# Low parts of four weight quarters in branch B computed on GpSimd instead of VectorE

## Chip, core and metric

One core of one Trainium2 chip runs the whole kernel. Times are device microseconds (us) of one execution; the number compared is the median over runs. TensorE is called PE, VectorE DVE, ScalarE ACT, GpSimd POOL; SP is the engine that only issues transfers here.

## The reference, cut to what matters

A mixer layer over 512 tokens of width 1024: one wide projection of the normalized input gives twelve blocks of 1024 columns, three branches (A: gated chunk mixing, B: window pooling, C: short convolution) use them, each branch is projected, gated and summed, and a last projection and norm follow.

```python
h = rmsnorm(x, norm_g[l])
proj = jnp.einsum('bsd,dn->bsn', h, w_in[l])
a_u, a_v, a_z, b_p, b_z, c_h, c_b, c_c, c_z, gate_logits = jnp.split(proj, SPLIT_OFFSETS, axis=-1)
...
yb = multiscale_pool(b_p, pool_w[l], pool_b[l], pool_scale[l]) * jax.nn.silu(b_z)
...
gates = jax.nn.sigmoid(gate_logits.reshape(bsz, s, N_BRANCH, D_MODEL))
merged = (gates[:, :, 0] * jnp.einsum('bsc,cd->bsd', ya, w_branch_a[l])
          + gates[:, :, 1] * jnp.einsum('bsc,cd->bsd', yb, w_branch_b[l])
          + gates[:, :, 2] * jnp.einsum('bsc,cd->bsd', yc, w_branch_c[l]))
```

## The kernel before

Everything is kept transposed, channels in partitions and tokens along the free dimension. Float32 accuracy comes from splitting each operand in a high part, which ACT makes by a rounding copy, and a low part, the difference between operand and high part, which DVE makes (`split`, lines 57 to 60). A product then takes three matmuls: high by high, high weights by low activations, low weights by high activations.

Most blocks of w_in are multiplied in `group` (lines 426 to 495), 512 output columns at a time, by a scheme of the Strassen kind with seven instead of eight quarter products. A group loads four weight quarters of 512 rows by 256 columns (tiles of 128x1024: a11, a12, a21, a22) and, in s1, the sum of two quarters, which an accumulating transfer from the POOL queue makes (line 469). DVE forms differences of quarters in place (line 457). The seven products, named by the activation form that they use, come in this order: b11, b21, t2, t1, t3, then b22 (from a12) and t4 (from a22, the quarter as loaded). Each is 24 matmuls at line 444 (2 column halves x 4 row blocks x 3 parts); within one row block the low weight part comes last in the code. `halved` (line 434) takes a high tile and a low tile, each from a pool of four, and calls `split`.

`run` (line 497) lets groups overlap: the first product of a group is issued before b22 and t4 of the group ahead of it. Branch B's list (lines 731 to 736) is: pool_in(1) with the window sums pools(1) behind it, pool_z(0), pool_mms(0), pool_z(1), gates(0), pool_mms(1), mixes(0), gates(1), mixes(1). pools (line 665) is DVE work: repeated shifted adds (line 677), a scaled difference (line 680), a short correction (lines 683 and 684), and a split. pool_mms multiplies by pool_w (lines 105 to 107) and ends in an epilogue on DVE and ACT (lines 706 to 709) whose results are needed in mixes. The results of a group are collected by DVE from PSUM (line 454) and by ACT (lines 450 and 524).

Only instructions wrapped in `pin` keep the order of the code. All others are ordered on each engine by a planner before the run, by the order of the code and by when it reckons each to be ready. Transfers of weights are issued by SP in its own order (line 64), seven raw weight tiles being in turn.

Of the kernel before, what the change touches and what calls it, by code (L numbers as in the profile page):

```python
# [8 lines left out]
F32 = mybir.dt.float32  # L9
F32R = mybir.dt.float32r  # L10
AF = mybir.ActivationFunctionType
ALU = mybir.AluOpType
# [14 lines left out]
OFF = {n: i * D for i, n in enumerate(["au", "av", "az", "bp", "bz", "ch", "cb", "cc", "cz", "g0", "g1", "g2"])}  # L27
# [3 lines left out]
def mixers_kernel(ctx, tc, x, norm_g, w_in, sgu_ln_g, sgu_ln_b, sgu_w, sgu_b, pool_w, pool_b, pool_scale,  # L31
                  conv_w, conv_b, w_branch_a, w_branch_b, w_branch_c, w_out, final_g, out):
    nc = tc.nc
# [20 lines left out]
    def bank():  # L54
        return psum.tile([P, 512], F32, tag="ps", name="ps")

    def split(hi, lo, src, keep=lambda ins: ins):

        keep(nc.scalar.copy(out=hi, in_=src))  # L59
        keep(nc.vector.tensor_tensor(out=lo, in0=src, in1=hi.bitcast(F32), op=ALU.subtract))  # L60

    def load_raw(src, shape):
        raw = wraw.tile([P, *shape], F32, tag="wraw", name="wraw")
        nc.sync.dma_start(out=raw, in_=src)
        return raw
# [8 lines left out]
    def cols(w2d, c0):  # L74

        v = w2d[:, c0 : c0 + GC].rearrange("(k p) c -> p k c", p=P)
        units = [load_w(v[:, 4 * h : 4 * h + 4, :], [4, GC]) for h in range(2)]

        def at(k, j):
            hi, lo = units[k // 4]  # L80
            return hi[:, k % 4, j * P : (j + 1) * P], lo[:, k % 4, j * P : (j + 1) * P]

        return at
# [319 lines left out]
    def proj(w, j, rhs_hi, rhs_lo, nk=KT):  # L403
        ps = bank()
        for k in range(nk):
            mm3(ps, w(k, j), (rhs_hi[:, k, :], rhs_lo[:, k, :]), k == 0, k == nk - 1)
        return ps

    def tile512(name):
        return tmp.tile([P, PAD + S], F32, tag="tmp", name=name)[:, 0:S]  # L410

    def out_tile(name):

        return outs.tile([P, 2, 2, S], F32, tag="outs", name=name)
# [8 lines left out]
    def pair_of(ap):  # L423
        return ap.rearrange("p (j t) -> p j t", j=2)

    def group(c0, g, ct, use=None):
        def source(kh, nh):
            c = c0 + nh * HALF + g * GC
            return w_in[kh * HALF : (kh + 1) * HALF, c : c + GC].rearrange("(k p) c -> p k c", p=P)

        def quarter(kh, nh):
            return load_raw(source(kh, nh), [4, GC])

        def halved(raw):
            hi = whi.tile([P, 4, GC], F32R, tag="whi", name="whi")
            lo = wlo.tile([P, 4, GC], F32R, tag="wlo", name="wlo")
            split(hi, lo, raw)
            return hi, lo

        def product(a, b, ps, first):  # L440
            for j in range(2):
                for k in range(4):
                    for n, (x, y) in enumerate([(0, 0), (0, 1), (1, 0)]):
                        nc.tensor.matmul(ps[:, j * GC : (j + 1) * GC], lhsT=a[x][:, k, j * P : (j + 1) * P],  # L444
                                         rhs=moving[b][y][:, k, :], start=first and j == 0 and k == 0 and n == 0,
                                         stop=k == 3 and n == 2, skip_group_check=True)

        def copied(ps):
            s = part.tile([P, S], F32, tag="part", name="part")
            nc.scalar.copy(out=s, in_=ps)  # L450
            return pair_of(s)

        def plus(half, ts, s, ps):
            nc.vector.tensor_tensor(out=ct[:, half, :, ts], in0=pair_of(ps), in1=s, op=ALU.add)  # L454

        def sub(out, in0, in1, op=ALU.subtract):
            nc.vector.tensor_tensor(out=out, in0=in0, in1=in1, op=op)  # L457

        a11 = quarter(0, 0)
        f = halved(a11)  # L460
        px, py, pz = bank(), None, None
        product(f, "b11", px, True)
        yield
        c1 = copied(px)
        a12 = quarter(1, 0)
        f = halved(a12)
        s1 = wsum.tile([P, 4, GC], F32, tag="wsum", name="s1")
        nc.sync.dma_start(out=s1, in_=source(0, 1))
        nc.gpsimd.dma_start(out=s1, in_=source(1, 1), accum_op=ALU.add)  # L469
        a21, a22 = quarter(0, 1), quarter(1, 1)  # L470
        py = bank()
        product(f, "b21", py, True)
        plus(0, T1, c1, py)
        sub(a21, a11, a21)
        sub(a11, s1, a11)
        product(halved(a11), "t2", px, False)
        c2 = copied(px)
        pz = bank()
        product(halved(s1), "t1", pz, True)
        product(halved(a21), "t3", px, False)  # L480
        c3 = copied(px)
        sub(a12, a12, a11)
        plus(1, T2, c3, pz)
        yield
        product(halved(a12), "b22", pz, False)
        plus(0, T2, c2, pz)
        if use:
            use(ct[:, 0], 0, slice(0, S))
            use(ct[:, 1, :, T2], 1, T2)
        product(halved(a22), "t4", px, False)  # L490
        if use:
            use(pair_of(px), 1, T1)
        else:
            nc.scalar.copy(out=ct[:, 1, :, T1], in_=pair_of(px))
        yield
# [26 lines left out]
    def act_into(ct, func):  # L522
        def use(src, half, ts):
            nc.scalar.activation(out=ct[:, half, :, ts], in_=src, func=func)
        return use
# [52 lines left out]
    def m_quarter(k, th):  # L578
        return merged[:, 4 * k : 4 * k + 4, th * GC : (th + 1) * GC]

    def form(name, src):

        m_form[name] = form_tile("m", f"f{len(m_form)}")
        split(*m_form[name], src)
# [8 lines left out]
    def merge(br, w_branch):  # L593

        state = {}

        def gates(g):
            state[g] = out_tile("gate")
            yield from group(OFF[f"g{br}"], g, state[g], act_into(state[g], AF.Sigmoid))

        def mixes(g):
            wb = {}

            def mix(t):
                if t % 2 == 0:
                    wb[t // 2] = cols(w_branch, t * P)
                return proj(wb[t // 2], t % 2, y_hi, y_lo)

            def under(t, ps):
                nonlocal merged  # L610
                if merged is None:
                    merged = acts.tile([P, KT, S], F32, tag="big", name="merged")
                gate = state[g][:, t // 4, t % 2]
                if br == 0:
                    nc.vector.tensor_mul(out=merged[:, t, :], in0=ps, in1=gate)
                    return
                pr = tile512("pr")
                nc.vector.tensor_mul(out=pr, in0=ps, in1=gate)
                nc.vector.tensor_add(out=merged[:, t, :], in0=merged[:, t, :], in1=pr)
                if br == 2 and g == 1 and t == 3:  # L620
                    form("b11", m_quarter(0, 0))
                    minus(m_quarter(0, 0), m_quarter(0, 0), m_quarter(0, 1))
                    form("-t1", m_quarter(0, 0))

            first = mix(TILES[g][0])

            def after():
                under(TILES[g][0], first)
                for t in TILES[g][1:]:
                    under(t, mix(t))  # L630

            return after

        for g in range(2):
            items.append(("group", gates(g), None))
            items.append(("other", lambda g=g: mixes(g)))
# [4 lines left out]
    def make_pads():  # L641
        for i in range(2):
            pads.append(const.tile([P, 2, PAD + S], F32, tag=f"pad{i}", name=f"ppad{i}"))
            nc.gpsimd.memset(pads[i][:, :, 0:PAD], 0.0)
# [11 lines left out]
    silu_z = {}  # L656

    def pool_in(g):
        if not pads:
            make_pads()  # L660
        yield from group(OFF["bp"], g, Padded())

    early = {}

# [26 lines left out]

    def pool_z(g):
        silu_z[g] = out_tile("sz")
        yield from group(OFF["bz"], g, silu_z[g], act_into(silu_z[g], AF.Silu))

    def pool_mm(p):
        hi, lo = load_w(pool_w[0, p].rearrange("(k p) c -> p k c", p=P), [2, GC])
# [130 lines left out]
    def product(units, name, pss, first):  # L828
        for b in range(2):
            for k in range(4):  # L830
                hi, lo = units[k // 2]
                for n, (x_, y_) in enumerate([(0, 0), (0, 1), (1, 0)]):
                    nc.tensor.matmul(pss[b], lhsT=m_form[name][x_][:, k, b * P : (b + 1) * P],  # L833
                                     rhs=(hi, lo)[y_][:, k % 2, :], start=first and k == 0 and n == 0,
                                     stop=k == 3 and n == 2, skip_group_check=True)
# [34 lines left out]
    px, pz = banks(), banks()  # L870
# [54 lines left out]
```

## Time and profile before

| | us |
|---|---|
| median of 3 runs | 702.45 |
| lowest and highest | 701.51, 703.87 |
| the profiled execution | 701.71 |
| its span | 699.9 |
| PE busy | 684.6 (98%) |
| DVE busy | 530.6 (76%) |
| ACT busy | 343.3 (49%) |
| POOL busy | 53.4 (8%) |

The span is the stretch from the first to the last instruction of the profiled execution; the rest of its time lies around it. PE's clock was granted in full (9 tenths or more in all but the last of the 40 slices). The rows of a timeline give start, duration, engine, line, operation, output and inputs, and in brackets how long the engine had been idle before and what ended that. An instruction's duration can reach a little into the next one's on the same engine.

### The profile page before, as it was taken

The numbers are of one execution on the slowest core, as the hardware profiler recorded it, in microseconds if no ns is written. First come the engines' busy times: TensorE is split into PE (matmuls) and PEld (weight loads), VectorE is DVE, ScalarE is ACT, GpSimd is POOL, SyncE is SP. The second block draws the span as 40 slices with busy tenths as digits, with TensorE's granted clock in tenths as the row PEclk, the third lists the DMA queues.
The fourth block names the chain that finished last, engine by engine and source line by source line (L and its number), as shares of the span: only waits on it lengthen the run. The fifth ranks groups of instructions, "written<-read, shape, count | busy, mean of one in ns | idle before, by whom it ended". The sixth has DMA issues, their size and how long they took to land.

```text
span 699.9 us, 11608 instructions
## 1 busy us (share of the span) xinstructions
PE 684.6 (98%) x4814; PEld 637.2 (91%) x4814; DVE 530.6 (76%) x615; ACT 343.3 (49%) x417; POOL 53.4 (8%) x68
## 2 busy tenths in 40 slices
PE   8999999999999999989999999999999999999994
PEld 6779999999899899989989899999999999898883
DVE  6997679695669667995855666798869975646995
ACT  7543546664244344655614334555645465244553
POOL 3112000000000000000000000000000000002112
PEclk9999999999999999999999999999999999999998
DMA  7974344746265434627617235556665543278733
GB/s 275 309 169 120 121 122 102 213 109 181 79 163 152 149 87 132 175 90 195 197 32 209 91 104 167 149 144 167 176 168 163 163 140 124 81 270 189 149 60 121
DMA packets 94457, 105.12 MB, mean 150 GB/s; under 512 B 3324, under 2 KB 85316, under 8 KB 94404
## 3 DMA queue, kind: packets, MB, share of 16 engines
q1 hardware_dynamic: 80020, 87.60, 38.9%
q0 software_dynamic: 13792, 15.73, 14.4%
q10 hardware_dynamic: 592, 1.05, 0.4%
q8 instruction: 37, 0.61, 0.4%
q14 instruction: 16, 0.13, 0.1%
HBM read 102.27 MB, written 2.10 MB: 149 GB/s over the span
## 4 chain that ended last, share of the span: by engine, by line
PE 89%; DVE 5%; DMA 2%; ACT 1%; issue 1%; POOL 0%; SPq 0%; POOLq 0%; ACTq 0%; DVEq 0%
PE ps L444 58%; PE ps L106 8%; PE ps L107 8%; PE ps L105 8%; PE ps L833 5%; PE ps L265 2%; DVE wlo L60 1%; DMA x_in<-in_x 1%; DVE win L677 1%; DMA wraw<-in_w_in 1%; DVE wraw L457 1%; PE ps L563 1%; PE ps L215 0%; DVE sz L454 0%; DVE ylo L709 0%
## 5 line engine op out<-in xcount | busy, mean ns | idle before, releaser
L59 ACT CAST whi<-wraw 128x1024 fp32r<-128x1024 f32 (+1 forms) x174 | 180.6, 1040 | 262.0 <-PE ps L444 160.2
L60 DVE TENSOR_TENSOR wlo<-wraw,whi 128x1024 fp32r<-128x1024 f32 (+1 forms) x174 | 209.6, 1210 | 95.6 <-ACT whi L59 95.3
L105 PE MATMUL ps<-yhi,whi 128*128 128x512 f32 x208 | 81.0, 389 | 0.0
L107 PE MATMUL ps<-yhi,wlo 128*128 128x512 f32 x208 | 80.9, 389 | 0.0
L106 PE MATMUL ps<-ylo,whi 128*128 128x512 f32 x208 | 80.9, 389 | 0.0
L457 DVE TENSOR_TENSOR wraw<-wraw 128x1024 f32<-128x1024 f32 x44 | 53.4, 1220 | 16.3 <-DMA wraw<-in_w_in 16.3
L469 POOL DMA_DIRECT2D s<-in_w_in x22 | 28.8, 1308 | 482.1 <-DMA s<-in_w_in 81.9
L444 PE MATMUL ps<-b22h,whi 128*128 128x256 f32 x176 | 50.6, 288 | 0.5 <-DVE sz L454 0.5
L444 PE MATMUL ps<-b21h,wlo 128*128 128x256 f32 x176 | 49.4, 280 | 1.2 <-DVE wlo L60 1.2
L444 PE MATMUL ps<-t2h,wlo 128*128 128x256 f32 x176 | 49.4, 281 | 0.5 <-DVE wlo L60 0.5
L444 PE MATMUL ps<-t1h,whi 128*128 128x256 f32 x176 | 49.4, 281 | 0.4 <-ACT whi L59 0.4
L444 PE MATMUL ps<-t2h,whi 128*128 128x256 f32 x176 | 49.5, 281 | 0.1
L444 PE MATMUL ps<-t2l,whi 128*128 128x256 f32 x176 | 49.6, 282 | 0.0
L444 PE MATMUL ps<-b11l,whi 128*128 128x256 f32 x176 | 49.6, 282 | 0.0
L444 PE MATMUL ps<-t3l,whi 128*128 128x256 f32 x176 | 49.6, 282 | 0.0
L444 PE MATMUL ps<-t1l,whi 128*128 128x256 f32 x176 | 49.6, 282 | 0.0
L444 PE MATMUL ps<-b22l,whi 128*128 128x256 f32 x176 | 49.6, 282 | 0.0
L444 PE MATMUL ps<-t4l,whi 128*128 128x256 f32 x176 | 49.6, 282 | 0.0
L444 PE MATMUL ps<-b21l,whi 128*128 128x256 f32 x176 | 49.6, 282 | 0.0
L444 PE MATMUL ps<-t3h,whi 128*128 128x256 f32 x176 | 49.3, 280 | 0.0
L444 PE MATMUL ps<-b22h,wlo 128*128 128x256 f32 x176 | 49.3, 280 | 0.0
L444 PE MATMUL ps<-b21h,whi 128*128 128x256 f32 x176 | 49.3, 280 | 0.0
(224 smaller groups left out, 1849.6 us busy)
## 6 DMA issues: line engine op xcount, KB each, us to landing
wraw<-in_w_in SPq DMA_DIRECT2D x96, 512.0 KB, 4.0
s<-in_w_in SPq DMA_DIRECT2D x22, 512.0 KB, 3.6
s<-in_w_in POOLq DMA_DIRECT2D x22, 512.0 KB, 6.3
wraw<-in_w_out SPq DMA_DIRECT2D x10, 512.0 KB, 3.8
wraw<-in_w_branch_a SPq DMA_DIRECT2D x8, 512.0 KB, 3.7
wraw<-in_w_branch_b SPq DMA_DIRECT2D x8, 512.0 KB
wraw<-in_w_branch_c SPq DMA_DIRECT2D x8, 512.0 KB
wraw<-in_w_out POOLq DMA_DIRECT2D x8, 512.0 KB, 6.0
```

Source lines behind the costliest of these rows:

```text
L59: keep(nc.scalar.copy(out=hi, in_=src))
L60: keep(nc.vector.tensor_tensor(out=lo, in0=src, in1=hi.bitcast(F32), op=ALU.subtract))
L105: nc.tensor.matmul(ps, lhsT=a[0], rhs=b[0], start=first, stop=False)
L106: nc.tensor.matmul(ps, lhsT=a[0], rhs=b[1], start=False, stop=False)
L107: nc.tensor.matmul(ps, lhsT=a[1], rhs=b[0], start=False, stop=last)
L265: pin(nc.tensor.matmul(vps[b], lhsT=a, rhs=r, start=done[b] == 1, stop=done[b] == 3 * KT))
L444: nc.tensor.matmul(ps[:, j * GC : (j + 1) * GC], lhsT=a[x][:, k, j * P : (j + 1) * P], rhs=moving[b][y][:, k, :], start=first and j == 0 a ...
L457: nc.vector.tensor_tensor(out=out, in0=in0, in1=in1, op=op)
L469: nc.gpsimd.dma_start(out=s1, in_=source(1, 1), accum_op=ALU.add)
L563: nc.tensor.matmul(mx[:, n * P : (n + 1) * P], lhsT=v_t[:, n, t * P : (t + 1) * P], rhs=wsT[:, t, :], start=True, stop=True)
L677: nc.vector.tensor_add(out=nxt[:, lo:], in0=cur[:, lo:], in1=cur[:, lo - step : PAD + S - step])
L833: nc.tensor.matmul(pss[b], lhsT=m_form[name][x_][:, k, b * P : (b + 1) * P], rhs=(hi, lo)[y_][:, k % 2, :], start=first and k == 0 and n == 0,
```

## The change

`split` takes an engine for the subtraction, DVE where none is named. `group` takes a `helper`, which goes to the split of a22 alone, the quarter of product t4. Four groups name GpSimd: gates(0) of branch B, pool_in(1), pool_z(0) and pool_z(1). All other splits, all shapes, buffers and values stay as they are.

```diff
-    def split(hi, lo, src, keep=lambda ins: ins):
+    def split(hi, lo, src, keep=lambda ins: ins, eng=None):
 
         keep(nc.scalar.copy(out=hi, in_=src))
-        keep(nc.vector.tensor_tensor(out=lo, in0=src, in1=hi.bitcast(F32), op=ALU.subtract))
+        keep((eng or nc.vector).tensor_tensor(out=lo, in0=src, in1=hi.bitcast(F32), op=ALU.subtract))
...
-    def group(c0, g, ct, use=None):
+    def group(c0, g, ct, use=None, helper=None):
...
-        def halved(raw):
+        def halved(raw, eng=None):
             hi = whi.tile([P, 4, GC], F32R, tag="whi", name="whi")
             lo = wlo.tile([P, 4, GC], F32R, tag="wlo", name="wlo")
-            split(hi, lo, raw)
+            split(hi, lo, raw, eng=eng)
             return hi, lo
...
-        product(halved(a22), "t4", px, False)
+        product(halved(a22, helper), "t4", px, False)
...
-            yield from group(OFF[f"g{br}"], g, state[g], act_into(state[g], AF.Sigmoid))
+            yield from group(OFF[f"g{br}"], g, state[g], act_into(state[g], AF.Sigmoid),
+                             helper=nc.gpsimd if br == 1 and g == 0 else None)
...
-        yield from group(OFF["bp"], g, Padded())
+        yield from group(OFF["bp"], g, Padded(), helper=nc.gpsimd if g else None)
...
-        yield from group(OFF["bz"], g, silu_z[g], act_into(silu_z[g], AF.Silu))
+        yield from group(OFF["bz"], g, silu_z[g], act_into(silu_z[g], AF.Silu), helper=nc.gpsimd)
```

## Rows read from the trace of the kernel before

**Rows 1.** The page: busy time by engine; the chain that ended last, by engine.

```profile
PE 684.6 (98%) x4814; PEld 637.2 (91%) x4814; DVE 530.6 (76%) x615; ACT 343.3 (49%) x417; POOL 53.4 (8%) x68
...
PE 89%; DVE 5%; DMA 2%; ACT 1%; issue 1%; POOL 0%; SPq 0%; POOLq 0%; ACTq 0%; DVEq 0%
```

**Rows 2.** Table by stage: stretch, length, busy us (instructions) of each engine, clock, transfers.

```profile
273.00:300.00 27.00, 27.00 (x210) 26.05 (x209) 26.93 (x47) 16.06 (x22) 1.29 (x1) 1.00 0.55 154
300.00:307.00 7.00, 4.79 (x34) 3.96 (x33) 6.93 (x9) 4.56 (x6) 0.00 (x0) 1.00 0.00 0
...
316.00:340.00 24.00, 24.00 (x193) 23.34 (x192) 15.06 (x17) 14.34 (x19) 1.29 (x1) 1.00 0.84 218
...
sum 632.00, PE 629.11 PEld 593.06 DVE 477.76 ACT 305.39 POOL 39.23; mean PE 78.64 PEld 74.13 DVE 59.72 ACT 38.17 POOL 4.90
```

**Rows 3.** Timeline of PE, 291 to 312 us: start, duration, engine, line, operation.

```profile
291.85 0.28 PE L444 MATMUL ps<-t4h,whi 128*128 128x256 f32 x1
...
297.40 0.28 PE L444 MATMUL ps<-b11h,whi 128*128 128x256 f32 x1
...
300.22 0.28 PE L444 MATMUL ps<-b21h,whi 128*128 128x256 f32 x1
...
301.86 0.39 PE L444 MATMUL ps<-b21h,wlo 128*128 128x256 f32 x1 [1.24 <-DVE wlo L60]
...
305.69 0.39 PE L444 MATMUL ps<-t1h,whi 128*128 128x256 f32 x1 [0.43 <-ACT whi L59]
...
306.69 0.38 PE L444 MATMUL ps<-t2h,wlo 128*128 128x256 f32 x1 [0.49 <-DVE wlo L60]
...
311.98 0.28 PE L444 MATMUL ps<-t3h,whi 128*128 128x256 f32 x1
```

**Rows 4.** Timeline of DVE, 261 to 306 us.

```profile
261.81 1.23 DVE L60 TENSOR_TENSOR wlo<-wraw,whi 128x1024 fp32r<-128x1024 f32 x1 [0.35 <-ACT whi L59]
264.63 1.23 DVE L60 TENSOR_TENSOR wlo<-wraw,whi 128x1024 fp32r<-128x1024 f32 x1 [1.59 <-ACT whi L59]
...
283.81 1.23 DVE L60 TENSOR_TENSOR wlo<-wraw,whi 128x1024 fp32r<-128x1024 f32 x1
...
285.55 1.23 DVE L60 TENSOR_TENSOR wlo<-wraw,whi 128x1024 fp32r<-128x1024 f32 x1
286.69 0.70 DVE L680 SCALAR_TENSOR_TENSOR d<-win,ppad 128x512 f32<-128x512 f32 x1
...
288.08 0.69 DVE L454 TENSOR_TENSOR sz<-ps,part 128x512 f32<-128x512 f32 x1
...
295.36 0.75 DVE L706 SCALAR_TENSOR_TENSOR y<-ps,pvec,sz 128x512 f32<-128x512 f32 x1
...
300.59 1.22 DVE L60 TENSOR_TENSOR wlo<-wraw,whi 128x1024 fp32r<-128x1024 f32 x1
...
305.42 1.22 DVE L60 TENSOR_TENSOR wlo<-wraw,whi 128x1024 fp32r<-128x1024 f32 x1
```

**Rows 5.** Timeline of ACT, two casts of pool_z(0).

```profile
280.78 1.05 ACT L59 CAST whi<-wraw 128x1024 fp32r<-128x1024 f32 x1 [2.26 <-PE ps L444]
...
283.59 1.05 ACT L59 CAST whi<-wraw 128x1024 fp32r<-128x1024 f32 x1 [0.76 <-ACT part L450]
```

**Rows 6.** Timeline of POOL: its subtraction, two pow operations, two accumulating loads.

```profile
12.79 2.40 POOL L236 TENSOR_TENSOR wlo<-wraw,whi 128x1024 fp32r<-128x1024 f32 x1 [0.54 <-ACT whi L232]
15.15 0.55 POOL L152 TENSOR_TENSOR rstd<-ms,mhalf 128x1 f32<-128x1 f32 x1
19.74 1.46 POOL L152 TENSOR_TENSOR rstd<-ms,mhalf 128x1 f32<-128x1 f32 x1 [4.04 <-DVE ms L199]
...
279.27 1.29 POOL L469 DMA_DIRECT2D s<-in_w_in  x1 [18.80 <-DMA s<-in_w_in]
313.66 1.30 POOL L469 DMA_DIRECT2D s<-in_w_in  x1 [33.09 <-DVE wraw L457]
```

**Rows 7.** Timeline of DVE at the second of these pow operations.

```profile
19.58 1.22 DVE L337 TENSOR_TENSOR hsum<-b21h,b21l 128x1024 f32<-128x1024 f32 x1
```

## The prediction

> **What bounds the kernel now.** I read the page's busy shares and its chain first, then PE by stage, then the one stage in which PE stands still. PE is busy 98% of the span and carries 89% of the chain that ended last; DVE carries 5% of it [rows 1]. The table by stage makes this sharp: from 20 to 652 us PE is busy 629.11 of 632 us, so 2.9 us of idle time is all there is, and 2.21 of it (7.00 less 4.79) lies between 300 and 307 us [rows 2]. There DVE is the engine that is late: it is busy 26.93 of the 27 us before and 6.93 of the 7 us of the hole [rows 2]. In the code this is branch B: the window sums of pools(1) and the epilogue of pool_mms(0) run on DVE while PE goes through pool_z(0), pool_mms(0) and the start of pool_z(1).
>
> The records of PE show what the hole costs in full. In pool_z(1) product b11 starts at 297.40 and b21 at 300.22, so one product of 24 matmuls takes 2.82 us. Undisturbed, t3, four products behind b11, would start at 297.40 + 4 x 2.82 = 308.68; it starts at 311.98. The loss is 3.30 us: PE stops for the low part of b21 (301.86), for a cast (305.69) and for the low part of t2 (306.69) [rows 3]. Those low parts are DVE's operations at 300.59 and 305.42, and PE goes on within 0.05 us of their ends (300.59 + 1.22 = 301.81; 305.42 + 1.22 = 306.64) [rows 3, 4]. So DVE time spent between 273 and 305 us is worth its length in kernel time, up to 3.30 us; DVE time spent elsewhere in branch B is worth nothing, because PE is full there.
>
> **What the change takes from DVE.** Four subtractions of 128x1024, one in each of pool_in(1), pool_z(0), pool_z(1) and gates(0) of branch B. Back to back, such an operation moves DVE on by 286.69 - 285.55 = 1.14 us [rows 4]. Each has to be placed:
> - pool_in(1): weight tiles come free four products back, and counting casts against products puts its low part at 261.81 or 264.63. DVE idles 1.59 us before the second of these [rows 4], so nothing late there is made earlier: 0.
> - pool_z(0): the casts of its b22 and t4 quarters are those at 280.78 and 283.59 [rows 5]; a12 comes first in the code, so t4's low part is the DVE operation at 285.55 [rows 4]. It lies in the unbroken DVE stretch ahead of both waits: -1.14 us. This is the only one of the four that can pay.
> - pool_z(1): its t4 cast needs the weight tile of t2, which PE takes up in earnest only at 306.69 [rows 3], after the last stop: 0.
> - gates(0): in 316 to 340 us DVE is busy 15.06 of 24 us and PE all 24 [rows 2]: 0.
>
> If nothing else happened, PE would stop 3.30 - 1.14 = 2.16 us instead of 3.30.
>
> **What it adds on GpSimd.** The trace has one such subtraction on GpSimd: 2.40 us at 12.79 [rows 6], 1.18 us longer than DVE's 1.22. Does t4 of pool_z(0) wait for it? The cast at 283.59 ends at 284.64; started then, the low part is there at about 287.1. PE reads it first in t4's third matmul, 291.85 + 0.24 = 292.09 [rows 3]. Cover: 5.0 us. The other three are covered more amply, since PE reads t4 a product or more behind their casts.
>
> GpSimd's own queue carries the accumulating loads of line 469. In the stretch they stand at 279.27 and 313.66 [rows 6]; between them the queue is empty for 33 us, so the subtraction of pool_z(0) waits for none of them and none for it. The one at 313.66 may come 2.4 us later behind the subtraction of pool_z(1); what it loads is the s1 of a group two ahead, so that costs 0. The raw quarter's buffer is given back about 1.2 us later, and SP loads the next weights into it; no PE wait in the stretch comes from a load: 0.
>
> **What GpSimd does to DVE** is the open price, and it decides the sign. Rows of before: GpSimd's one-element pow at 15.15 takes 0.55 us, the one at 19.74 takes 1.46 us [rows 6]; under the second, DVE runs a subtraction with both inputs in SBUF from 19.58 to 20.80 [rows 7], and GpSimd ends 0.40 us behind it. So GpSimd's reads wait for such a DVE operation. Whether DVE waits as well when GpSimd came first no row shows: under the 2.40 us at 12.79 DVE ran only operations with one input in PSUM. Bounds: at the low end DVE never waits, and the subtraction of pool_z(0) is worth -1.14. At the high end DVE waits for the whole 2.40 us, -1.14 + 2.40 = +1.26. I take a wait, because the one pair of rows that touches the question shows the two engines taking turns and not sharing. Its length: GpSimd goes on for 0.40 us after it had its data (the tail behind 20.80), so it holds DVE for 2.40 - 0.40 = 2.0 us. Behind the held instruction all of DVE's queue waits: the window sums, then the low parts of b11, b21 and t2 of pool_z(1), for which PE waits. Net on the path: -1.14 + 2.0 = +0.86 us.
>
> The Trainium skill ("SBUF — State Buffer", section "Who interferes with whom") says that a VectorE instruction with two SBUF inputs and a GpSimd instruction that reads SBUF exclude each other, and that the one that starts first keeps the other out for its whole length. The trace agrees for GpSimd kept out (1.46 against 0.55 us); for VectorE kept out no run here shows it. By that rule the sum would be +1.26 us, the high end above.
>
> The same hold can happen in the other three groups. There DVE has its own idle time, 9 of 24 us in gates(0)'s stretch [rows 2], and PE has no wait, so I put them at 0; without that cover each would cost what pool_z(0)'s does.
>
> **The sum.** The profiled execution took 701.71 us, 699.9 of span and 1.8 around it; the median of the three runs is 702.45, 0.74 above. Added to the profiled time, +0.86 gives 702.57; I add it to the median, which is what is compared: 703.3 us.
>
> **Rivals.**
> 1. DVE isn't held: -1.14, 701.3 us. For it: GpSimd may only get its reads in where DVE reads PSUM (the operation at 288.08 [rows 4] does, and 288.08 + 2.4 = 290.5 is still ahead of 292.09). Against it: the operations that follow there again have two SBUF inputs.
> 2. The planned order closes the hole: the order of DVE's work comes out of a planner, and with an operation less it may put the low part of b21 ahead of the pool epilogue (from 295.36 on [rows 4]), which PE doesn't need soon. At best all 3.30 go: 699.2 us. For it: more than 1.14 us of such movable work stands ahead of 300.59. Against it: code order put it there before, and nothing in the change alters the code order.
> 3. Slower: GpSimd is starved. DVE is back to back from 273 to 307, and nearly all of it reads two SBUF inputs. If GpSimd is kept out through 288.08 and gets in only at the pool epilogue, 295.36 [rows 4], its result is there at 295.36 + 2.40 = 297.76 and PE, which wants it at 292.09, stops for 5.67 us. DVE catches up meanwhile, so the old 3.30 us go: net +2.4, 704.8 us. It decides from the point where the low part lands later than 292.09 + 3.30 = 295.4; up to there the stop only changes its place. Against it: DVE reads PSUM at 288.08.
> 4. The change does not act on the path: pool_z(0)'s low part isn't the one at 285.55 but one outside the full DVE stretch. Then nothing moves: 702.45 us.
>
> **How the numbers follow.** Held (my forecast) 0.42; not held 0.26; hole closed 0.12; starved 0.14; no effect 0.06. A measurement of this kernel tells about 0.3% (2.1 us) from no change: the three runs span 701.51 to 703.87. Forecast, not held and no effect (0.74 together) lie within 2.1 us of 702.45, less some 0.06 that the scatter of runs carries over either bound. Faster by over 0.3% is the closed hole with a little of not held: 0.14. Slower is starvation and the upper tail of my forecast: 0.18. Same: 0.68. The range goes from 700.3 (not held, 701.3, less 1 us of run scatter; it leaves the closed hole out) to 705.8 (starved, 704.8, plus 1 us). Both signs hold much of the chance; the forecast's own range is 702.3 (hold of 1.0 us) to 704.7 (1.26 plus 1 us of scatter).
>
> **What would show it.** Right: in the table by stage PE's idle time stays in one hole of 2 to 5 us at about 300 to 308 us; GpSimd shows four 128x1024 subtractions, the second starting at about 285 and lasting 2.4 to 3.6 us; a DVE operation with two SBUF inputs beside it lasts about 2 us longer than its kind. If DVE's operations keep their lengths, rival 1 is right. If PE's longest wait is for GpSimd at t4 near 292, rival 3. If no PE wait for DVE is left and the pool epilogue stands behind the low part of b21, rival 2. The prediction is wrong in its ground if time moves in a stage before 273 or after 316 us, where I see none to gain or lose.

## The result, and the profile after

The changed kernel takes 707.97 us (median of 7 runs, 704.85 to 710.32) against 702.46 before: the ratio is 1.0066, with a 95% interval of 1.0048 to 1.0083. It is slower, by 3.4 to 5.8 us. A second measurement gave 1.0069 (1.0045 to 1.0093). The forecast was 703.3 us with a range up to 705.8. The ratios here and below leave out one execution, 749.92 us of the kernel with all but pool_z(0), whose granted clock was 0.85 on the mean.

The profiled execution took 707.97 us with a span of 706.2. First the table by stage of the changed kernel, same columns and stretches as [rows 2]:

```profile
273.00:300.00 27.00, 25.14 (x190) 24.33 (x189) 26.01 (x41) 14.14 (x18) 6.22 (x2) 0.94 0.56 157
300.00:307.00 7.00, 7.00 (x50) 6.49 (x50) 6.83 (x11) 4.26 (x7) 0.00 (x0) 1.00 0.00 0
307.00:316.00 9.00, 7.49 (x63) 7.29 (x63) 8.10 (x8) 4.93 (x6) 0.00 (x0) 1.00 0.41 133
316.00:340.00 24.00, 22.71 (x194) 22.51 (x194) 12.59 (x12) 11.51 (x14) 6.48 (x4) 1.00 0.71 172
```

Where one hole stood at 300 to 307 us, there are three: 1.86 us in the first row, 1.51 in the third, 1.29 in the fourth. In the first row PE's clock, ahead of the DMA columns, is 0.94 where it was 1.00. The timeline of PE names what ended each:

```profile
292.90 0.39 PE L444 MATMUL ps<-b22h,whi 128*128 128x256 f32 x1 [1.86 <-DVE sz L454]
...
310.74 0.39 PE L444 MATMUL ps<-t2h,wlo 128*128 128x256 f32 x1 [1.51 <-DVE wlo L60]
...
323.28 0.38 PE L444 MATMUL ps<-b22h,whi 128*128 128x256 f32 x1 [1.29 <-DVE sz L454]
```

Two of the three are for sz: the sum of line 454 (`plus(1, T2, c3, pz)`), which reads the PSUM bank that b22 then adds to. GpSimd's four subtractions, on its timeline:

```profile
266.55 2.40 POOL L60 TENSOR_TENSOR wlo<-wraw,whi 128x1024 fp32r<-128x1024 f32 x1 [4.58 <-ACT whi L59]
...
286.60 4.91 POOL L60 TENSOR_TENSOR wlo<-wraw,whi 128x1024 fp32r<-128x1024 f32 x1 [4.05 <-ACT whi L59]
...
318.62 2.91 POOL L60 TENSOR_TENSOR wlo<-wraw,whi 128x1024 fp32r<-128x1024 f32 x1
...
338.57 2.40 POOL L60 TENSOR_TENSOR wlo<-wraw,whi 128x1024 fp32r<-128x1024 f32 x1 [3.87 <-ACT whi L59]
```

And DVE at the second and the third of them:

```profile
286.82 0.68 DVE L678 TENSOR_TENSOR win<-win 128x513 f32<-128x513 f32 x1
287.42 1.22 DVE L457 TENSOR_TENSOR wraw<-wraw 128x1024 f32<-128x1024 f32 x1
288.56 0.68 DVE L681 SCALAR_TENSOR_TENSOR d<-win,ppad 128x512 f32<-128x512 f32 x1
289.16 2.38 DVE L684 TENSOR_TENSOR dh<-win,rcount 128x16 f32<-128x16 f32 x1
...
292.16 0.68 DVE L454 TENSOR_TENSOR sz<-ps,part 128x512 f32<-128x512 f32 x1
...
320.05 2.57 DVE L60 TENSOR_TENSOR wlo<-wraw,whi 128x1024 fp32r<-128x1024 f32 x1 [2.56 <-ACT whi L59]
322.54 0.68 DVE L454 TENSOR_TENSOR sz<-ps,part 128x512 f32<-128x512 f32 x1
```

In pool_z(0) GpSimd is ready at 286.60 and is kept out while three DVE operations pass; then it gets in, and the next DVE operation, 16 elements wide, lasts 2.38 us. It ends at 291.54, GpSimd at 291.51. It is the same DVE operation in all six traces in which GpSimd has pool_z(0)'s low part; why GpSimd gets in there and not earlier stays open. In pool_z(1) GpSimd starts while DVE is idle, and the DVE subtraction at 320.05 lasts 2.57 instead of 1.22 us [rows 4]. Behind each held operation stands sz, and for sz PE waits. In the other two groups GpSimd takes its 2.40 us, as in [rows 6], while DVE stands idle.

Start times of the same products in both traces give the account. The stretch from b11 of pool_in(1) to b11 of the second gates group of branch B took 367.70 - 252.17 = 115.53 us before and 372.99 - 254.03 = 118.96 after, 3.43 more:

| piece of the stretch | before | after | difference |
|---|---|---|---|
| b11 of pool_in(1) to b22 of pool_z(0) | 36.85 | 38.87 | +2.02 |
| to b11 of pool_z(1) | 8.38 | 10.05 | +1.67 |
| to t3 of pool_z(1) (the old hole) | 14.58 | 13.11 | -1.47 |
| to b22 of pool_z(1) | 5.91 | 7.22 | +1.31 |
| to b11 of the second gates group | 49.81 | 49.71 | -0.10 |

The second piece holds no wait but the fall of the clock. The table of the changed kernel in steps of 2 us shows it (the granted clock is the third number from the right; 0.50 of full speed is 1.2 GHz):

```profile
290.00:292.00 2.00, 1.04 (x5) 0.54 (x3) 2.00 (x2) 0.00 (x0) 1.51 (x1) 1.00 0.02 8
292.00:294.00 2.00, 1.10 (x9) 1.10 (x10) 2.00 (x6) 1.71 (x2) 0.00 (x0) 1.00 0.65 205
294.00:296.00 2.00, 2.00 (x13) 2.00 (x13) 2.00 (x5) 1.76 (x3) 0.00 (x0) 0.59 0.20 66
296.00:298.00 2.00, 2.00 (x12) 2.00 (x12) 2.00 (x4) 0.92 (x1) 0.00 (x0) 0.55 0.75 226
298.00:300.00 2.00, 2.00 (x19) 2.00 (x19) 2.00 (x4) 1.71 (x3) 0.00 (x0) 1.00 0.10 36
```

PE works again from 292.90 at the upper level, falls to the lower near 294.4 and is back by 298: 12 and 13 matmuls per 2 us instead of 19.

Of the 6.3 us between the two spans, 3.43 lie in this stretch, 1.86 ahead of it, 0.95 behind the last matmul (10.39 us from its start to the end, 9.44 before). The piece ahead is scatter: in the twelve traces of this study b11 of pool_in(1) started anywhere from 251.64 to 256.79 us, and at 252.26 in a second trace of the changed kernel itself. Most of it is PE's idle time between 20 and 44 us, long before the change: 1.50 us in this trace, 0.31 in the second, 0.11 in the trace of before. The piece at the end comes back below.

### The profile page after: what moved, and what is told of

Its sections match the earlier page's. It is cut to its first block, busy times and chain, and to the rows that moved or that the text cites. A ratio compares the mean times of both kernels' runs of the same rounds, so it can differ in the third digit from the quotient of the medians.

```text
span 706.2 us, 11614 instructions
## 1 busy us (share of the span) xinstructions
PE 685.6 (97%) x4814; PEld 638.1 (90%) x4814; DVE 529.5 (75%) x611; ACT 343.4 (49%) x417; POOL 65.8 (9%) x72
## 4 chain that ended last, share of the span: by engine, by line
PE 89%; DVE 4%; DMA 3%; ACT 2%; issue 1%; SPq 0%; POOL 0%; POOLq 0%; ACTq 0%; DVEq 0%
PE ps L444 59%; PE ps L106 8%; PE ps L107 8%; PE ps L105 8%; PE ps L834 5%; DMA ws_bs<-in_sgu_w 1%; DMA x_in<-in_x 1%; DVE wlo L60 1%; DMA wraw<-in_w_in 1%; PE ps L265 1%; DVE win L678 1%; PE ps L563 1%; PE ps L215 0%; DVE sz L454 0%; DMA out_y<-o 0%
## 5 line engine op out<-in xcount | busy, mean ns | idle before, releaser
L60 DVE TENSOR_TENSOR wlo<-wraw,whi 128x1024 fp32r<-128x1024 f32 x170 | 205.9, 1217 | 100.2 <-ACT whi L59 100.0
L444 PE MATMUL ps<-t4h,whi 128*128 128x256 f32 x176 | 49.5, 281 | 0.0
L444 PE MATMUL ps<-t4h,wlo 128*128 128x256 f32 x176 | 49.4, 281 | 0.0
```

The source lines that it names most:

```text
L60: keep((eng or nc.vector).tensor_tensor(out=lo, in0=src, in1=hi.bitcast(F32), op=ALU.subtract))
```

## The experiments

All read the stretch of branch B as above, in one trace each; ratios are from repeated runs.

| kernel | stretch, us | last matmul to end, us | ratio (95%) |
|---|---|---|---|
| before | 115.53 | 9.44 | 1 |
| changed | 118.96 | 10.39 | 1.0066 (1.0048 to 1.0083) |
| changed, second time | 119.34 | 10.40 | 1.0069 (1.0045 to 1.0093) |
| pool_z(0) alone | 117.68 | 9.50 | 1.0024 (1.0005 to 1.0043) |
| all but pool_z(0) | 116.27 | 9.70 | 1.0024 (1.0006 to 1.0041) |
| pool_in(1) and gates(0) | 115.54 | 9.47 | 1.0007 (0.9990 to 1.0024) |
| GpSimd only writes | 114.21 | 10.35 | 1.0000 (0.9981 to 1.0020) |
| epilogue later, no GpSimd | 112.37 | 9.47 | 0.9953 (0.9935 to 0.9971) |

**Which group costs: pool_z(0) alone.**

```diff
-             helper=nc.gpsimd if br == 1 and g == 0 else None)
+             helper=None)
-    yield from group(OFF["bp"], g, Padded(), helper=nc.gpsimd if g else None)
+    yield from group(OFF["bp"], g, Padded(), helper=None)
-    ... act_into(silu_z[g], AF.Silu), helper=nc.gpsimd)
+    ... act_into(silu_z[g], AF.Silu), helper=None if g else nc.gpsimd)
```

> Only pool_z(0) keeps its low part on GpSimd. Theory (GpSimd holds DVE): in the changed kernel DVE's tiny operation at 289.16 lasted 2.38 instead of about 0.18 us while GpSimd read, DVE's sum sz behind it came late, PE stood 1.86 us before b22, and PE's clock fell behind that. All of this is pool_z(0)'s, so most of the loss returns here: ratio 1.003 to 1.005 (2 to 3.5 us), with the long DVE operation and the PE wait for sz. Rival (the loss is spread over the groups, or comes from elsewhere in the run): about a quarter of it, ratio 1.000 to 1.002.

The stretch grew by 2.15 us, 63% of the changed kernel's 3.43; the ratio, 1.0024, lies below the 1.003 expected, and its interval is wide. The trace repeats the picture: a held operation of 2.37 us, GpSimd's subtraction 5.01 us long, PE waiting 1.95 us for sz, its clock at 0.50 between 292 and 294. So do the pieces of the table above: +2.01, +1.65, -1.49, -0.04 and +0.02 us. By the stretch the largest part is pool_z(0)'s.

**The other three.** The edit is the reverse: `helper=nc.gpsimd if g else None` for pool_z, the other two as in the change.

> The three other groups use GpSimd, pool_z(0) uses DVE. Theory: the hole of 3.3 us at 300 to 307 us is as in the kernel before, since nothing is held ahead of it; pool_z(1)'s subtraction can still hold DVE by up to 1.4 us ahead of the sum that b22 of pool_z(1) waits for: ratio 1.000 to 1.002, no fall of PE's clock. Rival (each of the four costs alike): 1.004 to 1.006.

The stretch grew by 0.74 us, all of it ahead of b22 of pool_z(1); the line of PE in that trace:

```profile
319.19 0.39 PE L444 MATMUL ps<-b22h,whi 128*128 128x256 f32 x1 [0.69 <-DVE sz L454]
```

The ratio, 1.0024, is just above the expected 1.002; what the trace shows, 0.74 us in the stretch and 0.26 at the end, would be 1.0014, inside the interval. The clock did not fall. By the ratios alone the two halves of the change cost the same, 1.0024 each; that pool_z(0) costs most rests on the stretch, in one trace of each kernel.

**The two groups in which DVE idles.** `helper=None` for pool_z, the other two as in the change.

> Only pool_in(1) and gates(0) use GpSimd, the two groups in which DVE has idle time. Theory: both are free, ratio within 0.999 to 1.001, GpSimd's two subtractions last 2.4 us each and no DVE operation beside them is longer than its kind. Rival (GpSimd at work costs wherever it stands, or later weight loads are pushed): 1.002 or more.

As expected: 115.54 us against 115.53, and no DVE operation there is longer than its kind: DVE stood idle all through GpSimd's two. GpSimd's work is free where DVE has nothing to do.

**GpSimd without its reads.** The same places and the same order; a fill stands for the subtraction.

```diff
-        keep((eng or nc.vector).tensor_tensor(out=lo, in0=src, in1=hi.bitcast(F32), op=ALU.subtract))
+        keep(eng.memset(lo.bitcast(F32), 0.0) if eng else nc.vector.tensor_tensor(out=lo, in0=src, in1=..., op=ALU.subtract))
```

> The changed kernel with GpSimd's four subtractions replaced by a fill with zeros of the same tiles: the low part of a22 is left out of the product t4 in these four groups. Waits and the order on every engine are those of the changed kernel, GpSimd only no longer reads SBUF. Theory (GpSimd's reads hold DVE): no DVE operation is lengthened, PE doesn't wait for sz, the clock stays up, and the removed DVE work shows as -1.1 us or a little more: ratio 0.997 to 1.000. Rival (the planner's new order, or the later hand-over from GpSimd to PE, makes the loss): the loss stays, 1.004 to 1.007.

The DVE order in the stretch is the changed kernel's, instruction for instruction. The waits are not quite: the fill reads no high part, so it doesn't wait for the cast, and it starts 31.41 us behind b11 of pool_in(1) where the subtraction started 32.57 behind it. The fill, the DVE subtraction beside it, the operation that was held before, and sz:

```profile
288.20 0.96 POOL L60 MEMSET wlo<- 128x1024 f32 x1 [2.64 <-PE ps L444]
...
288.43 1.22 DVE L60 TENSOR_TENSOR wlo<-wraw,whi 128x1024 fp32r<-128x1024 f32 x1
...
291.91 0.17 DVE L684 TENSOR_TENSOR dh<-win,rcount 128x16 f32<-128x16 f32 x1
...
292.69 0.69 DVE L454 TENSOR_TENSOR sz<-ps,part 128x512 f32<-128x512 f32 x1
```

0.17 instead of 2.38 us, and the DVE subtraction beside the fill takes its usual 1.22 us: the fill neither holds DVE nor is held. sz starts 35.90 us behind b11 of pool_in(1), against 35.91 before and 38.13 in the changed kernel. PE doesn't wait for sz in the stretch, the clock stays up there, and the stretch is 114.21 us, 1.32 shorter than before and 4.75 shorter than with the subtraction. So the planner's new order doesn't make the loss. Nor does the hand-over: in no trace does PE wait for GpSimd in the stretch. What is left is the subtraction. The fill is shorter (0.96 us where the subtraction takes 2.40), but it holds DVE not at all. It leaves out the arithmetic together with the reads; no run here parts these two. The ratio, 1.0000, is at the upper edge of what was expected: the end is 0.91 us longer, as in the changed kernel, and takes back most of the gain.

**Half the reads.** On the kernel with pool_z(0) alone:

```diff
+        if eng:
+            keep(eng.tensor_tensor(out=lo[:, 0:2], in0=src[:, 0:2], in1=hi[:, 0:2].bitcast(F32), op=ALU.subtract))
+            keep(eng.memset(lo[:, 2:4].bitcast(F32), 0.0))
+            return
```

> As the run with pool_z(0) alone on GpSimd, but GpSimd subtracts only half of the tile (128x512) and fills the other half with zeros: half of a22's low part is left out of t4. Order on PE, DVE and ACT as in that run. There the held DVE operation lasted 2.37 us and PE then stood 1.95 us for sz. Theory (the hold is the length of GpSimd's read, and it alone delays sz): the held operation lasts 1.2 to 1.5 us, PE's wait for sz is 0.7 to 1.1 us, and its clock falls less or not at all. Rival (a fixed price per GpSimd operation, or a wait caused by the order): 2.2 us and 1.9 us again.

Here is the held operation on DVE:

```profile
287.69 1.29 DVE L688 TENSOR_TENSOR dh<-win,rcount 128x16 f32<-128x16 f32 x1
```

and what PE waits for behind it:

```profile
290.33 0.39 PE L448 MATMUL ps<-b22h,whi 128*128 128x256 f32 x1 [0.86 <-DVE sz L458]
```

Half the subtraction gives half the hold, as expected: 1.29 against 2.37 us, and the wait falls by as much, from 1.95 to 0.86. GpSimd's subtraction still lasts 3.92 us, from 285.02 to 288.94, but for some 2.7 of them it was kept out, since the held operation starts at 287.69. DVE pays for GpSimd's work, not for its waiting, and by its length, not at a fixed price per operation. The clock stayed up, and the stretch was 115.32 us.

**The clock.** On the kernel with pool_z(0) alone, spare work for PE behind the first product of pool_mms(0):

```diff
+        if g == 0:
+            spare = bank()
+            for _ in range(9):
+                nc.tensor.matmul(spare[:, 0:P], lhsT=ones, rhs=ones, start=True, stop=True)
```

> As the run with pool_z(0) alone on GpSimd, with nine spare matmuls of 128x128 on a matrix of ones put into PE's queue between the first product of pool_mms(0) and b22, so PE works through part of its wait for sz. In that run, b22 and t4 of pool_z(0) took 5.0 plus 1.0 us more than undisturbed, because the clock fell after the wait. Theory (the fall follows PE's standing still): PE's idle time before b22 shrinks below 0.6 us, the clock stays at the upper level, and b22 runs its 24 matmuls in about 3 instead of 4.6 us. Rival (the fall has nothing to do with the wait): b22 takes 4.6 us again. Later parts aren't compared, since the planner also moves the pool epilogue here.

PE's timeline (the nine matmuls are 18 records):

```profile
289.67 2.17 PE L721 MATMUL ps<-ones 128*128 128x128 f32 x18
291.68 0.39 PE L444 MATMUL ps<-b22h,whi 128*128 128x256 f32 x1
```

and its table in steps of 2 us:

```profile
290.00:292.00 2.00, 2.00 (x19) 1.97 (x18) 2.00 (x5) 0.92 (x2) 0.29 (x1) 1.00 0.21 52
292.00:294.00 2.00, 2.00 (x19) 2.00 (x18) 2.00 (x5) 1.99 (x3) 0.00 (x0) 1.00 0.62 210
```

DVE was held for 2.38 us and b22 came just as late, 38.86 us behind b11 of pool_in(1) in both, but PE wasn't idle ahead of it, and the clock is 1.00 where it was 0.50 in the run without spare work. b22 takes 3.1 instead of 4.6 us, and from b22 to b11 of pool_z(1) pass 8.52 us instead of 10.03. So the standing still costs about 1.5 us on top of itself. (The expectation's "5.0 plus 1.0 us more" is a misreading: b22 and t4 together took 7.29 us in the run without spare work and 5.66 in the kernel before, 1.63 more.)

**The old hole.** The hole of [rows 3] was worth 3.30 us. Nothing about GpSimd is in this kernel; it is the kernel before with the epilogue of pool_mms(0) put behind t3 of pool_z(1):

```diff
         def after():
+            if g == 0:
+                waiting.extend([first, pool_mm(g + 2)])
+                return
             first()
             pool_mm(g + 2)()
...
+    def with_waiting(gen):
+        next(gen)
+        yield
+        next(gen)
+        for f in waiting:
+            f()
+        yield
+        next(gen)
+        yield
...
-              ("group", pool_z(1), None)]
+              ("group", with_waiting(pool_z(1)), None)]
```

> The kernel before, without GpSimd's help, with the epilogue of pool_mms(0) issued after t3 of pool_z(1) in the code, so that the planner puts the low parts of pool_z(1) ahead of it on DVE. Theory (the 3.3 us hole of the kernel before is DVE time spent on work that PE doesn't need yet): the hole shrinks to under 1 us, the stretch from b11 of pool_in(1) to b11 of the second gates group falls from 115.5 to 112.3 to 113.5 us, ratio 0.995 to 0.998. Rival (PSUM banks held longer by the waiting sums, or the epilogue is late for its use, makes a new wait): 0.999 to 1.003.

It is faster than both kernels: 700.01 us against 703.25 for the kernel before beside it, ratio 0.9953. PE's row for the stage of the hole, and DVE with the low part of t2 ahead of three of the four epilogue products:

```profile
300.00:307.00 7.00, 7.00 (x58) 6.84 (x58) 7.00 (x8) 4.55 (x6) 0.00 (x0) 1.00 0.15 44
```

```profile
303.44 1.21 DVE L60 TENSOR_TENSOR wlo<-wraw,whi 128x1024 fp32r<-128x1024 f32 x1
...
308.11 2.05 DVE L706 SCALAR_TENSOR_TENSOR y<-ps,pvec,sz 128x512 f32<-128x512 f32 x3
```

PE's 2.21 idle us there [rows 2] are gone, and the stretch is 3.16 us shorter. DVE does as much as before (530.3 us busy in the whole kernel, 530.6 before), only in another order.

**The changed kernel again.**

> The changed kernel once more beside the others. In its first profile the stretch from b11 of pool_in(1) to b11 of the second gates group took 3.4 us longer than before, and 2.9 us more lay in the first 254 and the last 40 us, where the code and the order are the same. Theory: 3 to 4 us in the stretch again, the rest scatters from execution to execution: ratio 1.004 to 1.007. Rival (the start or the end is slower because of the change): ratio 1.008 or more, with the same extra in the first 254 us.

Stretch 119.34 us and ratio 1.0069, both as expected; the waits for sz 1.86 and 1.62 us, the end 10.40 us. The first 252 us were as in the kernel before, so the early 1.86 us of the first trace were scatter. The end was not: some 0.95 us longer in both.

**What lengthens the end.** Two kernels with the groups chosen anew: the first moves GpSimd's help from pool_z to the second gates group of branch B and the first of branch C, the second takes only gates(0) back to DVE.

```diff
-             helper=nc.gpsimd if br == 1 and g == 0 else None)
+             helper=nc.gpsimd if br == 1 or (br == 2 and g == 0) else None)
-    ... act_into(silu_z[g], AF.Silu), helper=nc.gpsimd)
+    ... act_into(silu_z[g], AF.Silu))
```

> Four low parts on GpSimd again, but in groups where DVE idles or PE waits for no sum: pool_in(1), both gates groups of branch B, the first gates group of branch C. In the changed kernel the time from the last matmul to the end was 10.4 us against 9.4 to 9.7 in the kernels with none to three such groups. If four GpSimd subtractions as such lengthen the end, it is about 10.4 us here too; if the end belongs to what pool_z(0) and pool_z(1) change together, it is 9.4 to 9.7. In the stretch of branch B the theory of the hold expects 115.3 to 115.8 us, as in the kernel before; a price per GpSimd operation would give over 116.5.

The stretch was 115.51 us, that of the kernel before. But only two of the four subtractions lie in it, so it says nothing on the third and the fourth. They stand at 385.31 and 586.42, and DVE was not idle all through them: beside each, an operation with two SBUF inputs was held, 2.25 and 2.50 us where its kind takes 1.22. The first pair:

```profile
385.31 2.39 POOL L60 TENSOR_TENSOR wlo<-wraw,whi 128x1024 fp32r<-128x1024 f32 x1 [6.72 <-ACT whi L59]
...
386.53 2.25 DVE L457 TENSOR_TENSOR wraw<-wraw 128x1024 f32<-128x1024 f32 x1 [2.89 <-DMA wraw<-in_w_in]
```

PE waited for nothing behind either: from b11 of the second gates group to the last matmul passed 322.84 us, against 322.76 before. So a hold is free where nobody waits for what stands behind it. The end was 9.20 us, so the number of subtractions doesn't lengthen it.

```diff
-             helper=nc.gpsimd if br == 1 and g == 0 else None)
+             helper=None)
```

> The changed kernel with gates(0) back on DVE: three low parts on GpSimd (pool_in(1), pool_z(0), pool_z(1)). The theory of the hold expects the whole loss in the stretch of branch B, 118.7 to 119.4 us against 115.5 before, since gates(0) was free. The end: 9.4 to 9.7 us if it takes all four groups, 10.4 us if pool_z(0) and pool_z(1) together are enough.

The end was 9.55 us. The stretch was longer than expected, 121.1 us: here the second wait for sz was 1.84 us, and the clock fell behind that one too.

```profile
322.49 0.38 PE L444 MATMUL ps<-b22h,whi 128*128 128x256 f32 x1 [1.84 <-DVE sz L454]
```

b22 of pool_z(1) then took 4.6 instead of 3.1 us. Three traces have the long end: the two of the changed kernel and that of the kernel in which GpSimd only writes, which share one program order; none of the others has it. In all three the last output transfer trails off on few DMA engines, at 27 GB/s in its last microsecond. Neither the number of GpSimd operations nor their reads explain it, and what does stays open. It is some 0.9 of the 4.6 us.

## Why the prediction was wrong, point by point

**The bound** was right as far as it went: PE, with 3.30 us lost to DVE work that came too early in its order. The run with the later epilogue took 3.16 us of it back. What did not follow from it is that "DVE time spent elsewhere in branch B is worth nothing, because PE is full there": a full PE shows that it doesn't wait yet, not how near it is to waiting.

**Which group matters** was half right. pool_in(1) and gates(0) are free (115.54 us). pool_z(1) was put at 0, because its low part lies behind the last stop for a low part and DVE idles there. It costs 1.31 us, since GpSimd, once started, holds DVE ahead of a sum. In the kernel before that sum was ready 0.05 us ahead of its use (317.16 + 0.68 = 317.84 against 317.89):

```profile
317.16 0.68 DVE L454 TENSOR_TENSOR sz<-ps,part 128x512 f32<-128x512 f32 x1
...
317.89 0.39 PE L444 MATMUL ps<-b22h,whi 128*128 128x256 f32 x1
```

**The hold** was right in kind and nearly in size: 2.0 us forecast; the held operation lasted 2.38 us, 2.2 more than its kind. The Trainium skill's rule ("SBUF — State Buffer", section "Who interferes with whom") is that the other engine is kept out for the whole instruction; with the 2.40 us of [rows 6] that is as near as my 2.0, one 0.2 us above, the other 0.2 below. The trace agrees in that the held operation ended 0.03 us behind GpSimd. It adds that the one waiting isn't always served next: three DVE operations passed GpSimd while it stood ready. (My reading of the 2.40 us at 12.79 had one slip: at 13.97 DVE also ran a 0.15 us operation with a single input in SBUF; it wasn't held either.)

**The step that failed** is "Behind the held instruction all of DVE's queue waits: the window sums, then the low parts", that is, the list of who waits. I followed DVE's late work to the one place where PE was already waiting, the low parts at 300 us, and so set the hold against the gain at that place (-1.14 + 2.0). But sz stands in the queue too, in pool_z(0) and again in pool_z(1), and b22 waits for it. In the kernel before it ended at 288.08 + 0.69 = 288.77 [rows 4], and b22 started at

```profile
289.02 0.28 PE L444 MATMUL ps<-b22h,whi 128*128 128x256 f32 x1
```

Cover: 0.25 us, which shows as no wait at all. So the hold reached PE 11 us earlier than I put it, at nearly its full length (+2.02), and at a place where the standing still was followed by a fall of the clock. The hold and the gain by themselves came out near the forecast (+2.02 - 1.47 = +0.55 against +0.86); what it lacked are pool_z(1)'s wait and the fall of the clock, both by way of sz, and the longer end.

**The gain of 1.14 us** did not stand ahead of sz: the planner filled the freed place with the subtraction at 287.42 (line 457), which had stood at 291.71. The gain showed later, in the smaller hole (-1.47, with PE itself later). In the run in which GpSimd only writes, the stretch has it in full: 1.32 us.

**The clock** was in no term. After the 1.86 us of standing still it added 1.67 us. It fell in all four traces with a first wait of 1.86 to 1.95 us for sz; after the waits of 1.29 and 1.62 us in pool_z(1) it did not fall, after 1.84 us there it did. The old hole had not shown it: [rows 2] have the clock at 1.00 there.

**The sum** by what was measured: +2.02 + 1.67 - 1.47 + 1.31 - 0.10 = 3.43 us, and 0.95 at the end, 4.4 us; the ratio gives 4.6. The forecast had +0.86 from the first and the third term and nothing for the others.

**The rivals.** Not held (-1.14) fell: DVE was held. Starved fell as well: GpSimd was kept out for 2.5 us only, and PE never waited for GpSimd. The closed hole didn't come by this change, but by another it is real: with the epilogue moved, -3.16 us of the 3.30. The slow case had its chance of 0.18 for the wrong reason. Of the signs that were named, the long DVE operation came. PE's idle time did not stay in one hole, GpSimd's second subtraction lasted 4.91 us and not 2.4 to 3.6, and time moved behind 316 us, which was to show that the ground is wrong.

## What to carry to other kernels

Before work is put on GpSimd beside a full DVE, list every result in DVE's queue that another engine waits for, with how long before its use it is ready, and not only the results that are late already: a cover of 0.25 us looks like no wait. Work with SBUF inputs moved from DVE to GpSimd was free here where DVE idled all through it, or where nobody waited for what stood behind the hold; where DVE was full it held DVE for 2.2 us, nearly twice what DVE needed for the work. Where the order of a full engine is the trouble, change the order: moving some 4.6 us of work that nobody needed yet behind the low part of t2 gained 3.2 us.

## What the runs showed of the hardware

- A DVE operation with two SBUF inputs was held while GpSimd subtracted two tiles in SBUF, even a small one: 128x16 lasted 2.38 us beside tiles of 128x1024 and 1.29 us beside half of them, and 0.17 us with no subtraction beside it. A GpSimd fill, which only writes, did not hold DVE: a DVE subtraction beside it took its usual 1.22 us.
- GpSimd was kept out by DVE as well, and not only by the operation in progress: its 2.40 us became 4.91, with three DVE operations passing in between.
- After PE's wait of 1.86 us its clock fell to the lower level near 294.4 us, though PE had been at work again since 292.90, and it was back at the upper by 298; with spare matmuls in place of the wait it didn't fall. In the run with pool_z(0) alone it fell sooner, in the same 2 us in which PE, at 291.08, went back to work (0.84 there). The changed kernel's times scattered from 704.85 to 710.32 us in 7 executions, against 701.39 to 706.05 in 35 of the kernel before.
